# Weight sums of the first layer's seven-product down step, made ahead by GpSimd in the pool mixer's stage

## The chip, the core and the metric

The kernel runs on one core of a Trainium2 chip. The metric is the device time of one execution in microseconds. Three runs of the kernel before took 3083.82, 3086.56 and 3086.64 us; the median is 3086.56 us.

## What is computed

The reference is a two-layer transformer on 1024 tokens of width 1024, in float32. The parts that matter here, cut to their core:

```python
# first layer
h = rms_norm(x, attn_norm_w)
y_pool = pool_mixer(u_pool, pool_w, pool_scale) @ w_pool_br      # pool mixer
y_attn = nsa_attention(q, k, v, nsa_g, ...) @ w_attn_br          # 16 heads, 32-token query blocks
x = x + (merge_g[:, :, 0] * y_pool + merge_g[:, :, 1] * y_attn) @ w_o
h = rms_norm(x, ffn_norm_w)
u = causal_conv3(h @ w_up)                                       # 2 x 2752 columns
gate, val = split(u)
x = x + (silu(gate) * val) @ w_down                              # 2752 x 1024
# second layer: another mixer, then
h = h + square(relu(rmsnorm(h) @ w_ff1)) @ w_ff2                 # 4096 columns
```

## The kernel before, in words

Every large product is done to float32 accuracy in three matmuls: each operand is split in a high part (ScalarE, `whi`) and a remainder (VectorE or GpSimd, `wlo`), and `mm3` (L98) adds high x high, high x low and low x high. Splits of weights are at L93 and L94 (`unit`) and at L912 and L913 (`split`).

The feed-forward products use Strassen's method in the seven-product form of Winograd: a block of 512 rows of `w_down` or `w_ff2` is cut in quarters, and instead of eight quarter products there are seven, of sums of quarters. `down_fast` (L957) does this for four tiles of activations at once. It needs four sums of activation quarters on every call (`put(A, ...)`, L971, GpSimd) and four sums of weight quarters. There are two forms of it. Without `sums`, it loads the quarters, some of them twice (L967, L1025, L1029), and GpSimd forms the four sums of 128x1024 in place: at L1026 and L1028, and by two `put(B, ...)` at L971. With `sums`, it loads ready sums from a DRAM tensor at L1005, each just before its split. The first layer calls `down_fast` four times, without sums (in `phase_ffn1`, L1245, a loop over `n`; the rest of `w_down` is done by plain products). The second layer calls it seven times with sums.

Those sums of the second layer come from a generator, `weight_sums` (L921). It goes in steps, four to a weight group, each over a quarter's 256 columns. A step issues on SP's queue the stores of the step before (L942) and the loads of the step after (L933), and has GpSimd form four sums (L945 to L948) of 128x256. It has four tags of tiles with three buffers each. It is driven from the second layer's mixer by `next_step`, and its last step stores at L953.

The order of work is made by a planner when the program is built: each engine and each DMA queue has its own instruction list and works it off in order, and among what is ready in the planner's clock it takes what stands first in the program. `issue_after(ins)` adds one rule: what the block issues on the engine of `ins` goes behind `ins` in that engine's list. If `ins` is a DMA on SP's queue, the block's DMAs on SP stand behind it, and its GpSimd work is not bound by it.

SBUF memory is a stack of pools. A pool opened after another was closed begins where that one began; its tiles take their place in the order in which they are created. With `reuse_waits="tile"` a new tile waits for the last uses of those old tiles that lie on its bytes.

The stages around the change, in order: keys and values, queries (`phase_q`), the pool mixer (`phase_pool`, L232), the attention (`phase_attn`, L478). `phase_pool` has small tables (`rcnt` 256 bytes a partition, `pw` 2048, `psc` 16), then `yph` and `ypl` (16 KB each), and ends in a loop over eight output tiles: 24 matmuls, a copy by ScalarE to `yp` (four buffers) and a store to `yp_d` (L283). `phase_attn` opens its pool `pattn` with `wmask` (1280 bytes, a GpSimd DMA), `cmask` (1024 bytes, a GpSimd DMA), `fold` (768 bytes, set by VectorE at L490), `ftab` (512 bytes) and the query tiles `qt0` (4 KB, two buffers) and `qt1`. Its first step loads queries (L500), and runs `compressed`: scores on TensorE (L506), minima on VectorE, products on GpSimd (L512, L521, L526), a selection mask `sm`; then the masked scores (L566 on VectorE). TensorE's other work there is the gates (`gate_filler`): sixteen pieces of it, that is four halves of 24 matmuls each, stand in the program ahead of the first step, and the others are put by `issue_after` behind a matmul of the attention.

Of the kernel before, what the change touches and what calls it, by code (L numbers as in the profile page):

```python
# [22 lines left out]
P = 128  # L23
# [200 lines left out]
def early_gate(k, xT, z, n, g_d):  # L224

    nc = k.nc
    nc.scalar.activation(z, k.fm(k.unit(k.a["w_g"][n], 1024, P), *xT), AF.Tanh, scale=0.5)
    nc.gpsimd.tensor_scalar(z, z, 0.5, 0.5, op0=OP.mult, op1=OP.add)
    nc.sync.dma_start(g_d[n // 8, n % 8], z)


def phase_pool(k, xT, yp_d, g_d):  # L232

    nc, a = k.nc, k.a
    xh, xl = xT
    with k.tc.tile_pool(name="ppool", bufs=2, reuse_waits="tile") as p:
        rcnt = p.tile([P, 4, 16], F32, name="rcnt", bufs=1)
        nc.scalar.dma_start(rcnt, a["c_rcnt"])
        pw = p.tile([P, 4, P], F32, name="pw", bufs=1)
        nc.scalar.dma_start(pw, a["pool_w"])  # L240
        psc = p.tile([P, 4], F32, name="psc", bufs=1)
        nc.scalar.dma_start(psc, a["pool_scale"])
        yh = p.tile([P, 4, T], F32R, name="yph", bufs=1)
        yl = p.tile([P, 4, T], F32R, name="ypl", bufs=1)
        def pooled(g):
            acc = k.fm(k.unit(a["w_u"][g], 1024, P), xh, xl)
            u = p.tile([P, T], F32, tag="u", name=k.nm("u"), bufs=1)
            nc.scalar.activation(u, acc, AF.Copy)
            s = u
            for i in range(g + 1):  # L250
                d = 1 << i
                s2 = p.tile([P, T], F32, tag="s", name=k.nm("s"), bufs=4)
                nc.vector.tensor_tensor(s2[:, d:], s[:, d:], s[:, :T - d], op=OP.add)
                nc.gpsimd.tensor_copy(s2[:, :d], s[:, :d])
                s = s2
            wd = 2 << g
            nc.vector.tensor_tensor(s[:, :wd], s[:, :wd], rcnt[:, g, :wd], op=OP.mult)
            nc.vector.scalar_tensor_tensor(s, s, 1.0 / wd, u, op0=OP.mult, op1=OP.subtract)
            return g, s

        def mixed(g, s):
            for h in range(2):
                hs = slice(h * 512, h * 512 + 512)
                pa = k.bank("o")
                nc.tensor.matmul(pa, pw[:, g, :], s[:, hs], start=True, stop=True)
                nc.scalar.activation(yh[:, g, hs], pa, AF.Copy, scale=psc[:, g:g + 1])
                nc.vector.scalar_tensor_tensor(yl[:, g, hs], pa, psc[:, g:g + 1], yh[:, g, hs].bitcast(F32),
                                               op0=OP.mult, op1=OP.subtract)
        late = None
        for g in range(3, -1, -1):  # L270
            late, this = pooled(g), late
            if this:
                mixed(*this)
        for n in EARLY[1:]:
            early_gate(k, xT, p.tile([P, T], F32, tag="s", name=k.nm("z"), bufs=4), n, g_d)
        mixed(*late)
        for n in range(8):
            if n % 2 == 0:
                wb = k.unit(a["w_pool_br"][n // 2], 1024, P)
            acc = k.fm(wb, yh, yl, (3, 2, 1, 0), 4 * (n % 2))  # L280
            y = p.tile([P, T], F32, tag="s", name=k.nm("yp"), bufs=4)
            nc.scalar.copy(y, acc)
            nc.sync.dma_start(yp_d[n], y)  # L283


def rope_const(k, p):
# [634 lines left out]
def weight_sums(k, p, w, dst, n):  # L921

    nc = k.nc
    tt = nc.gpsimd.tensor_tensor
    steps = [(g, slice(h * 256, h * 256 + 256)) for g in range(n) for h in range(4)]

    def load(g, s):
        q = {}  # L930
        for name, (j, c) in (("b22", (1, 1)), ("b12", (0, 1)), ("b11", (0, 0)), ("b21", (1, 0))):
            q[name] = p.tile([P, 256], F32, tag=name, name=k.nm(name), bufs=3)
            nc.sync.dma_start(q[name], w[2 * g + j][c][:, s])  # L933
        return q["b11"], q["b12"], q["b21"], q["b22"]

    made, now = None, load(*steps[0])
    after = yield
    for i, (g, s) in enumerate(steps):
        with k.tc.issue_after(after.ins):
            if made:  # L940
                for d, x in made:
                    nc.sync.dma_start(d, x)  # L942
            following = load(*steps[i + 1]) if i + 1 < len(steps) else None
            b11, b12, b21, b22 = now
            tt(b12, b22, b12, op=OP.subtract)  # L945
            tt(b11, b12, b11, op=OP.add)
            tt(b21, b11, b21, op=OP.subtract)
            tt(b22, b22, b11, op=OP.subtract)  # L948
            made, now = [(dst[g, j][:, s], x) for j, x in enumerate((b12, b11, b21, b22))], following
        after = yield  # L950
    with k.tc.issue_after(after.ins):
        for d, x in made:
            nc.sync.dma_start(d, x)  # L953
    yield
# [183 lines left out]
    return h[:, 0], h[:, 1]  # L1138


def phase_ffn1(k, xT, acc, out_d):


    nc, a = k.nc, k.a
    t1, t2 = slice(0, 512), slice(512, T)
    with k.tc.tile_pool(name="pffn1", bufs=1, reuse_waits="tile") as p:
# [20 lines left out]
        def new_pair():  # L1167
            return p.tile([P, 2, T], F32, tag="uv", name=k.nm("uv"), bufs=2)
# [48 lines left out]
        us = [new_pair()]  # L1217
# [18 lines left out]
        for n in range(4):  # L1236
            us = []
            for j in range(4):
                if j % 2 == 0:
                    us.append(new_pair())  # L1240
                fast(1 + 4 * n + j, us[-1][:, j % 2], x)
                if n == 0 and j == 1:
                    with k.tc.issue_after(k.last_sum.ins):
                        swap_basis(k, acc, True, nc.vector)
            down_fast(k, p, us, [a["w_down"][1 + 2 * n + j] for j in range(2)], acc)  # L1245
        us = []
        for j in range(4):
            if j % 2 == 0:
# [92 lines left out]
def next_step(steps, after):  # L1341
    try:
        steps.send(after)
    except StopIteration:
        pass
# [553 lines left out]
@with_exitstack  # L1899
def transformer_kernel(ctx, tc, a, out, dbg=None):  # L1900
    k = K(ctx, tc, a, out, dbg)
    nc = tc.nc
    d = lambda shape, name, dt=F32: k.dram.tile(shape, dt, name=name)
    yp_d, g_d = d([8, P, T], "yp_d"), d([2, 8, P, T], "g_d")
    q_d, m_d = d([2, NT, P, 1024], "q_d"), d([8, P, 512], "m_d")
    x2_d, x3_d, y_d = (d([T, T], n) for n in ("x2_d", "x3_d", "y_d"))
    a_d = d([8, P, T], "a_d")
    v_d = d([T, 512], "v_d")

    qk_d = d([4, 2, 2, P, T], "qk_d")  # L1910
    xT = k.xopen()
    with tc.tile_pool(name="pkv", bufs=1, reuse_waits="tile") as p:
        kT = p.tile([P, 4, T], F32R, name="kT")
        V = p.tile([P, NT, 4, P], F32R, name="V")
        gates = p.tile([P, NT, 48], F32, name="gates")
        kcm = p.tile([P, 2, 2, 64], F32R, name="kcm")
        vcm = p.tile([P, 2, 2, 64], F32, name="vcm")
        phase_kv(k, xT, kT, V, gates, kcm, vcm, g_d)
        phase_q(k, xT, q_d)
        phase_pool(k, xT, yp_d, g_d)  # L1920
        k.close_psum()
        aT = phase_attn(k, kT, V, gates, q_d, kcm, vcm, a_d, xT, yp_d, g_d, m_d)
        k.open_psum(True)
    with tc.tile_pool(name="pacc", bufs=1, reuse_waits="tile") as p:
        acc = p.tile([P, NT, T], F32, name="acc1")
        xT = phase_wo(k, aT, g_d, m_d, acc)
        xT = phase_ffn1(k, xT, acc, x2_d)
    ws_d = d([7, 4, P, 1024], "ws_d")
    with tc.tile_pool(name="pahead", bufs=1, reuse_waits="tile") as p:
        k.ahead = weight_sums(k, p, a["w_ff2"], ws_d, 7)  # L1930
        next(k.ahead)
        yT, pre = phase_mix(k, xT, x2_d, y_d, v_d, qk_d)
    k.open_psum(True)
    p = ctx.enter_context(tc.tile_pool(name="px", bufs=1, reuse_waits="tile"))
    xT = p.tile([P, KT, T], F32R, name="xTh"), p.tile([P, KT, T], F32R, name="xTl")
    phase_res(k, "w_out", "ln_ff_g", yT, x2_d, x3_d, xT, (4, 5, 6, 7, 0, 1, 2, 3), pre)
    k.xclose()
    with tc.tile_pool(name="pacc2", bufs=1, reuse_waits="tile") as p:
        acc = p.tile([P, NT, T], F32, name="acc2")
        phase_ffn2(k, xT, x3_d, acc, ws_d)  # L1940
    k.close_psum()
# [141 lines left out]
```

## Time and profile before

| | |
|---|---|
| median of 3 runs | 3086.56 us |
| profiled execution | 3091.48 us, span 3089.7 us, mean granted TensorE clock 0.986 |
| TensorE busy | 2946.4 us, 95% of the span |
| VectorE, ScalarE, GpSimd busy | 2078.6 us (67%), 1375.3 us (45%), 1186.6 us (38%) |
| DMA | 293.06 MB, 95 GB/s in the mean |
| pool mixer's loop over output tiles | about 304 to 342 us of the span |
| attention | from 341 us |
| first layer's seven-product down steps | four, the first from about 1318 to 1350 us, the others each 122 us later |
| `weight_sums` of the second layer | 28 steps, 1863 to 2018 us |

The profile is one execution taken by the hardware profiler; its times are microseconds from the start of the span. PE is TensorE, DVE is VectorE, ACT is ScalarE, POOL is GpSimd, SP is SyncE, and SPq its DMA queue's issuing side.

### The profile page before, as it was taken

How to read it: one execution, taken by the hardware profiler on the slowest of the kernel's cores; microseconds unless marked ns; L12 is line 12 of the kernel's file. 1: busy time of each engine (PE TensorE's matmuls, PEld its weight loads, DVE VectorE, ACT ScalarE, POOL GpSimd, SP SyncE). 2: the span in 40 equal slices, each digit the busy share in tenths (PEclk: the TensorE clock that was granted, in tenths of full speed). 3: DMA queues.
4: the chain of work that ended last, by engine and by line, in shares of the span. 5: the costliest groups of instructions: out<-in, count | busy, mean ns of one | idle time of the engine just before them, and what ended most of it. 6: DMA issues, size and time to landing. Idle time of an engine off the chain costs nothing. (4 is left out here: it accounts for less than half of the span.)

```text
span 3089.7 us, 41918 instructions
## 1 busy us (share of the span) xinstructions
PE 2946.4 (95%) x14822; PEld 2442.4 (79%) x14822; DVE 2078.6 (67%) x4005; ACT 1375.3 (45%) x2447; POOL 1186.6 (38%) x1007
## 2 busy tenths in 40 slices
PE   8999999999999898999999999899989999999998
PEld 7887789889888776777877787676777878888876
DVE  8495277877777689687777873442465766666667
ACT  5243266666667234444434442332363453333333
POOL 3032355544455520344243405811331034444452
PEclk9999999999999998999999999999999999999999
DMA  3232412221232510111211127721783312222223
GB/s 135 77 112 91 154 42 74 68 67 52 88 100 93 194 62 29 55 62 41 67 57 53 64 96 235 233 77 40 185 217 113 112 62 76 75 75 76 75 75 136
DMA packets 157362, 293.06 MB, mean 95 GB/s; under 512 B 47969, under 2 KB 87393, under 8 KB 157153
## 3 DMA queue, kind: packets, MB, share of 16 engines
q1 hardware_dynamic: 150528, 274.72, 28.2%
q10 hardware_dynamic: 5760, 13.28, 1.3%
q8 instruction: 117, 1.92, 0.3%
q0 software_dynamic: 864, 2.39, 0.2%
q14 instruction: 93, 0.75, 0.1%
HBM read 225.09 MB, written 65.54 MB: 94 GB/s over the span
## 5 line engine op out<-in xcount | busy, mean ns | idle before, releaser
L912 ACT ACTIVATE whi<-wraw 128x1024 fp32r<-128x1024 f32 (+1 forms) x220 | 217.0, 991 | 349.1 <-PE up L101 148.6
L913 DVE TENSOR_TENSOR wlo<-wraw,whi 128x1024 fp32r<-128x1024 f32 x208 | 274.1, 1323 | 34.7 <-ACT whi L912 32.8
L577 POOL TENSOR_SCALAR e<-e,den,gates 128x640 f32<-128x640 f32 (+7 forms) x256 | 199.0, 790 | 215.4 <-DVE den L575 177.6
L101 PE MATMUL o<-wlo,whi 128*128 128x512 f32 x688 | 271.7, 395 | 10.0 <-DVE wlo L913 8.8
L102 PE MATMUL o<-whi,wlo 128*128 128x512 f32 x688 | 266.9, 393 | 12.8 <-DVE wlo L913 12.8
L100 PE MATMUL o<-whi,whi 128*128 128x512 f32 x688 | 253.6, 396 | 18.5 <-ACT whi L912 8.3
L990 DVE TENSOR_TENSOR acc<-acc,o 128x512 f32<-128x512 f32 x320 | 209.6, 679 | 20.7 <-PE o L102 20.3
L591 ACT ACTIVATE eh<-tr 128x512 fp32r<-128x512 f32 (+1 forms) x304 | 158.2, 537 | 121.3 <-PE o L595 79.4
L592 DVE TENSOR_TENSOR el<-tr,eh 128x512 fp32r<-128x512 f32 (+1 forms) x304 | 183.1, 615 | 41.2 <-ACT eh L591 35.5
L1105 POOL TENSOR_TENSOR wraw<-wraw,wraw 128x512 f32<-128x512 f32 x34 | 48.0, 1412 | 421.2 <-DVE wlo L913 319.1
L570 ACT ACTIVATE e<-e,m 128x640 f32<-128x640 f32 (+7 forms) x256 | 187.1, 733 | 34.5 <-DVE m L566 28.9
L93 ACT ACTIVATE whi<-wraw 128x1024 fp32r<-128x1024 f32 (+2 forms) x109 | 113.4, 1045 | 176.1 <-PE o L102 29.0
L565 PE MATMUL s<-kT,qt 128*128 128x320 f32 (+5 forms) x768 | 184.3, 347 | 4.1 <-DVE m L566 3.9
L100 PE MATMUL up<-xh,whi 128*128 128x512 f32 x432 | 171.7, 398 | 0.6 <-ACT xh L158 0.6
L100 PEld LDWEIGHTS o<-whi,whi 128*128 128x128 f32 x688 | 130.7, 190 | 52.0 <-ACT whi L912 10.7
L102 PE MATMUL up<-xh,wlo 128*128 128x512 f32 x432 | 170.2, 396 | 0.0
L101 PE MATMUL up<-xl,whi 128*128 128x512 f32 x432 | 169.8, 394 | 0.0
L102 PEld LDWEIGHTS o<-whi,wlo 128*128 128x128 f32 x688 | 129.6, 189 | 44.4 <-DVE wlo L913 17.9
L101 PEld LDWEIGHTS o<-wlo,whi 128*128 128x128 f32 x688 | 130.9, 190 | 42.0 <-DVE wlo L913 13.7
L94 DVE TENSOR_TENSOR wlo<-wraw,whi 128x1024 fp32r<-128x1024 f32 (+2 forms) x86 | 125.6, 1465 | 55.7 <-ACT whi L93 55.1
L587 PE MATMUL tr<-ident,e 128*128 128x128 f32 x1056 | 158.8, 274 | 3.1 <-ACT et L532 1.5
L595 PE MATMUL o<-el,V 128*128 128x256 f32 x528 | 146.3, 299 | 7.2 <-DVE el L592 6.6
(489 smaller groups left out, 8482.8 us busy)
## 6 DMA issues: line engine op xcount, KB each, us to landing
wraw<-in_w_ff_dram SPq DMA_DIRECT2D x57, 512.0 KB, 3.2
wraw<-in_w_up_dram SPq DMA_DIRECT2D x43, 512.0 KB, 3.2
b<-in_w_ff_dram SPq DMA_DIRECT2D x112, 128.0 KB, 3.2
ws_d<-b SPq DMA_DIRECT2D x112, 128.0 KB, 2.8
wraw<-ws_d SPq DMA_DIRECT2D x28, 512.0 KB, 3.2
wraw<-in_w_down_dram SPq DMA_DIRECT2D x26, 512.0 KB, 3.2
nqk<-qk_d SPq DMA_DIRECT2D x48, 256.0 KB, 5.9
wraw<-in_w_g_dram SPq DMA_DIRECT2D x16, 512.0 KB, 3.6
```

The costliest lines, as they stand in the source:

```text
L100: mm(out, sh, mh, start=first, stop=False, **kw)
L101: mm(out, sh, ml, start=False, stop=False, **kw)
L102: return mm(out, sl, mh, start=False, stop=last, **kw)
L565: nc.tensor.matmul(s[:, :w], qs[i][:, h, :], kT[:, br * 2 + g, ks], start=(i == 0), stop=(i == 1))
L570: nc.scalar.activation(e[:, :W], e[:, :W], AF.Exp, bias=m[:, n - 1:n], scale=-1.0, accum_out=den)
L577: nc.gpsimd.tensor_scalar(es[j][:, :W], es[j][:, :W], den[:, j:j + 1], gt[:, j, br:br + 1], op0=OP.mult, op1=OP.mult)
L587: nc.tensor.transpose(pt[:, x:x + P], es[i][:, (c + j) * P:(c + j + 1) * P], k.ident)
L591: nc.scalar.activation(eh[:, :w], pt[:, :w], AF.Copy)
L592: nc.vector.tensor_tensor(el[:, :w], pt[:, :w], eh[:, :w].bitcast(F32), op=OP.subtract)
L912: k.last_split = (k.nc.scalar.activation(pair[0], x, AF.Copy), (engine or k.nc.vector).tensor_tensor(pair[1], x, pair[0].bitcast(F32), op= ...
L913: (engine or k.nc.vector).tensor_tensor(pair[1], x, pair[0].bitcast(F32), op=OP.subtract))
L990: nc.vector.tensor_tensor(o, o, banks[t], op=op)
```

## The change

The sums of the four first-layer steps are made by the same generator, `weight_sums`, with four groups, so 16 steps, and kept in a new DRAM tensor `wd_d`. The first step's loads are issued ahead of the pool mixer's stage. Behind each of the first seven `yp_d` stores of the loop two calls of the generator are queued, behind the eighth three; 17 calls are 16 steps and the last stores. `down_fast` gets `wd_d[n]` and takes its form with sums. The generator's pool, `pahead1`, is opened before `phase_pool` and closed after it, so that the mixer's pool lies above its 12 tiles of 1 KB a partition.

```diff
@@ phase_pool
-            nc.sync.dma_start(yp_d[n], y)
+            sent = nc.sync.dma_start(yp_d[n], y)
+            for _ in range(3 if n == 7 else 2):
+                next_step(k.ahead, sent)
@@ phase_ffn1
-def phase_ffn1(k, xT, acc, out_d):
+def phase_ffn1(k, xT, acc, out_d, wd_d):
-            down_fast(k, p, us, [a["w_down"][1 + 2 * n + j] for j in range(2)], acc)
+            down_fast(k, p, us, [a["w_down"][1 + 2 * n + j] for j in range(2)], acc, False, wd_d[n])
@@ transformer_kernel
+    wd_d = d([4, 4, P, 1024], "wd_d")
-        phase_pool(k, xT, yp_d, g_d)
+        with tc.tile_pool(name="pahead1", bufs=1, reuse_waits="tile") as pa:
+            k.ahead = weight_sums(k, pa, a["w_down"][1:], wd_d, 4)
+            next(k.ahead)
+            phase_pool(k, xT, yp_d, g_d)
-        xT = phase_ffn1(k, xT, acc, x2_d)
+        xT = phase_ffn1(k, xT, acc, x2_d, wd_d)
```

The generator's core, which is not changed (`load` issues four DMAs of 128x256 on SP and takes the tags in the order `b22`, `b12`, `b11`, `b21`):

```python
for i, (g, s) in enumerate(steps):
    with k.tc.issue_after(after.ins):
        if made:
            for d, x in made:
                nc.sync.dma_start(d, x)
        following = load(*steps[i + 1]) if i + 1 < len(steps) else None
        b11, b12, b21, b22 = now
        tt(b12, b22, b12, op=OP.subtract)
        ...
    after = yield
```

## Rows read from the trace of the kernel before

**Rows 1.** Waits, engine PE, the first layer's feed-forward: total us, times, longest.
```profile
PE o L101 <- DVE wlo L913: 8.1, 8, 1.4
PE o L100 <- ACT whi L912: 6.3, 4, 1.6
...
PE o L102 <- DVE wlo L913: 2.7, 4, 0.7
PE o L100 <- DVE acc L990: 2.3, 4, 0.6
```
**Rows 2.** Waits, engine PE, the second layer's seven down steps, 2490 to 2980 us.
```profile
PE o L102 <- DVE wlo L913: 8.9, 7, 1.7
```
**Rows 3.** Timeline, POOL, first down step: start us, busy us, line, operation, tiles.
```profile
1323.40 2.41 POOL L1028 TENSOR_TENSOR wraw<-wraw,wraw 128x1024 f32<-128x1024 f32 x1
1330.29 9.10 POOL L971 TENSOR_TENSOR uv<-uv,uv 128x1024 f32<-128x1024 f32 x3 [4.48 <-DVE uv L1165]
1339.35 6.72 POOL L971 TENSOR_TENSOR wraw<-wraw,wraw 128x1024 f32<-128x1024 f32 x2
```
**Rows 4.** Timeline, DVE, the same step.
```profile
1323.45 2.37 DVE L1153 SCALAR_TENSOR_TENSOR uv<-ends,convp,uv 128x1 f32<-128x1 f32 x1
```
**Rows 5.** Timeline, SP's DMA issues, from the mixer's loop to the attention.
```profile
305.13 0.33 SPq L283 DMA_DIRECT2D yp_d<-yp  x1
...
336.43 5.92 SPq L283 DMA_DIRECT2D yp_d<-yp  x2
342.46 5.12 SPq L500 DMA_DIRECT2D qt<-q_d  x6
```
**Rows 6.** Timeline, PE: first and last matmul of a gate half, first scores.
```profile
340.75 0.39 PE L100 MATMUL f<-xh,whi 128*128 128x512 f32 x1
...
346.01 0.40 PE L102 MATMUL f<-xh,wlo 128*128 128x512 f32 x1
349.60 1.97 PE L506 MATMUL s<-kcm,qt 128*128 128x128 f32 x8 [3.19 <-DMA qt<-q_d]
```
**Rows 7.** Timeline, POOL, from the loop to the first attention step.
```profile
332.99 0.75 POOL L485 DMA_DIRECT2D wmask<-in_c_wmask_dram  x1
...
360.15 0.62 POOL L738 TENSOR_SCALAR z<-z 128x512 f32<-128x512 f32 x1 [5.41 <-ACT z L737]
360.75 1.04 POOL L521 TENSOR_TENSOR ec<-ec,dc 128x512 f32<-128x512 f32 x1
```
**Rows 8.** Timeline, DVE, from the loop's end to the first masked score.
```profile
341.02 0.22 DVE L490 MEMSET fold<- 128x192 f32 x1 [41.39 <-PE mm L102]
...
356.36 0.20 DVE L518 RECIPROCAL dc<-dc 128x8 f32<-128x8 f32 x1
...
366.18 0.69 DVE L566 CUSTOM_DVE_ANT_0 e<-s,sm 128x512 f32<-128x512 f32 x1 [1.17 <-POOL sm L548]
```
**Rows 9.** Timeline, SP's DMA issues, second layer's `weight_sums`: three steps between these.
```profile
1890.65 1.87 SPq L933 DMA_DIRECT2D b<-in_w_ff_dram  x4
...
1902.30 2.08 SPq L933 DMA_DIRECT2D b<-in_w_ff_dram  x4
```
**Rows 10.** Timeline, POOL, second layer's `weight_sums`: steps 1, 10 and 28.
```profile
1866.22 0.74 POOL L945 TENSOR_TENSOR b<-b,b 128x256 f32<-128x256 f32 x1 [80.11 <-DMA b<-in_w_ff_dram]
...
1907.72 0.73 POOL L945 TENSOR_TENSOR b<-b,b 128x256 f32<-128x256 f32 x1
...
2013.80 0.73 POOL L945 TENSOR_TENSOR b<-b,b 128x256 f32<-128x256 f32 x1 [2.06 <-DMA b<-in_w_ff_dram]
```
**Rows 11.** DMA issues: tiles, count, KB each, median us from issue to landing.
```profile
b<-in_w_ff_dram SPq DMA_DIRECT2D x112, 128.0 KB, 3.2
ws_d<-b SPq DMA_DIRECT2D x112, 128.0 KB, 2.8
```
**Rows 12.** Windows: busy us of PE, PEld, DVE, ACT, POOL; granted clock, DMA share, GB/s.
```profile
1890.00:1900.00 10.00, 10.00 (x45) 8.05 (x44) 1.50 (x4) 0.37 (x1) 7.44 (x11) 1.00 0.82 252
```
**Rows 13.** Timeline, ACT: it reads the fourth gate half.
```profile
373.26 0.60 ACT L737 ACTIVATE z<-f 128x512 f32<-128x512 f32 x1 [2.64 <-PE f L102]
```

## The prediction, made before the run

> **What bounds the kernel now.** I read the busy shares first: TensorE works 95% of the span, so a change counts only by what it does to TensorE's idle time. Next, TensorE's waits in the two stretches that the change touches. In the first layer's feed-forward the four seven-product down steps each show the same five stops: 8.1 + 6.3 + 2.7 + 2.3 = 19.4 us in all, 4.85 us a step [rows 1]. In the second layer, whose seven steps already read their sums from DRAM, all that recurs is 8.9 us over seven waits, 1.27 us a step [rows 2]. Then the timeline of one of the four steps, to see whose the stops are. GpSimd makes the weight sums in two pairs, two of 2.41 us and two in 6.72 us, around three sums of activations of 9.10 us [rows 3]. During the first pair a VectorE operation on 128x1 elements takes 2.37 us and ends with the GpSimd add (1325.82 against 1325.81) [rows 3, 4]; the accumulates queued behind it are late, and TensorE waits for one of their banks [rows 1]. The second pair stands before the last weight splits and the last stop.
>
> Last, the place where the work goes. The pool mixer's loop over eight output tiles is full of TensorE work and nearly empty elsewhere: VectorE waits 41.39 us there, up to 341.02 [rows 8]. Its stores leave the SP queue at 305.13 and, the eighth, after 336.43 (two in 5.92 us, so at about 342.0) [rows 5]. Right behind it stands the start of the attention, which is not full: TensorE runs one gate half (24 matmuls, 340.75 to 346.41), then waits 3.19 us for the first `qt` [rows 6].
>
> **What goes.** In each of four steps, four adds of 128x1024 and two second loads of weights; four splits now take loaded sums. The price is the stops, 19.4 us, less what remains. I take the second layer's remainder, 4 x 1.27 = 5.1: gain 14.3 us. Bounds: 19.4 if nothing remains; 9 if the stops of 1.6 us that wait for a split behind the three activation sums [rows 1, 3] and about one other remain, since VectorE has the convolution beside it here and not in the second layer. A loss is excluded as far as rows go: the same routine with two more loads a step makes no DMA wait of TensorE in seven steps [rows 2].
>
> The Trainium skill, SBUF — State Buffer, "Who interferes with whom", says that a VectorE instruction with two SBUF inputs and a GpSimd one that reads SBUF shut each other out, whole. The 2.37 us row agrees. By that rule VectorE gets back more than the stops tell, the gain is the upper end, 19.4 us, and the forecast would be 5 us lower, 3097.
>
> **What comes.** 16 steps; each is four loads and four stores of 128 KB on SP's queue and four adds of 128x256 on GpSimd. One load group goes out ahead of the stage. The rest are queued behind the loop's stores: two calls behind each, three behind the eighth. GpSimd: 4 x 0.74 = 2.95 us a step, 47 us in all, beside the gates' splits; by itself it would nearly keep up. SP: where the second layer's steps run undisturbed, three take from 1890.65 to 1902.30, 3.88 us each for eight issues [rows 9]. After 305.13 there are 31 groups of four, 15.5 x 3.88 = 60 us, with some 12 other issues of 0.33 us or more (4 us, of the kind in [rows 5]): last issue at 369, and with 2.8 us to land [rows 11], 372. So SP alone is some 30 us late at the end of a loop of 37 us. Buffers and data cost more: in the second layer the first ten steps' adds begin from 1866.22 to 1907.72, nine intervals, 4.61 us each; all 28 to 2013.80 make 5.47 us [rows 10]. I take 4.61, the row nearest to a place where VectorE is idle and GpSimd nearly so. Step 1's adds can begin at 305.13 + 1.9 (four issues) + 3.2 (landing) = 310.2; step 15's then at 310.2 + 14 x 4.61 = 374.7; with 2.95 of adds, 0.4 to issue and 2.8 to land, the last sum is in DRAM at **L = 381**. As a check, 31 groups are 16.3 MB; at the 252 GB/s of 1890 to 1900 [rows 12] that is 64.5 us without the loop's own traffic, so 370 at the earliest. Bounds of L: 354 (load 15 may leave only behind the eighth store at 342.0: 1.9 + 3.2 + 2.95 + 3.2, rounded up), and 393 with 5.47.
>
> **Why L is on the path.** Tiles take their memory in order of creation from the base of the stage before. The trace shows it: the attention's `wmask` DMA leaves at 332.99 with the loop still running, since with `cmask` it covers 2.3 KB, where `rcnt`, `pw` and `psc` (2.3 KB) lay; the next tile, `fold`, waits for the loop's last matmul, because it lies on `yph`, and the `qt` load leaves at 342.46 [rows 5, 7, 8]. After the change the base is that of the sums' pool, 12 tiles of 1 KB. `wmask`, `cmask`, `fold` and `ftab` end at 3.5 KB, the first `qt` at 7.5 KB: it lies on all three buffers of `b12`, so on steps 13, 14 and 15. The attention can't load its first query before step 15's stores have landed. Queued in front of it on GpSimd is the `wmask` DMA, and behind that everything that the attention wants of GpSimd.
>
> From issue to first score matmul took 342.46 to 349.60, 7.1 us; then 16.6 us to the first masked score on VectorE at 366.18 [rows 5, 6, 8]. In that chain a GpSimd product whose input was ready at 356.56 started at 360.75, behind a gate's operation [rows 7, 8]: 4.2 us that go when the gates are done by then. TensorE has four gate halves (some 5.5 us each) ahead of the first step, and the later ones are pinned behind a matmul of the attention; ScalarE reads the fourth at 373.26, so it ran behind this stretch [rows 13], and drawn into it covers 5.5 us. The cost is L + 7.1 - 349.6 - 4.2 - 5.5 = **L - 352.2**: 29 us at 381, 41 at 393, 2 at 354. A start at a lower clock after a stop was there before too, so I add nothing for it. Other things at nothing: the loop's matmuls (VectorE's 41.39 us without work say that no weight is split there [rows 8], and four `yp` buffers give each store three more tiles' time), and the memory by which the mixer's tiles shift; if a store of the loop held up a fifth tile, it would cost a tile's time, 37 / 7 = 5.3 us [rows 5].
>
> **Sum.** 29 - 14.3 = +15 us. The profiled execution took 3091.48 us (span 3089.7), so 3106 for a like one; it was 4.9 us above the median of the runs, 3086.56, and the same difference gives **3102 us**.
>
> **Rivals.** (1) Faster: the sums hide. One mechanism: the steps run at GpSimd's pace, 2.95 us, because issues and landings overlap, so that only the pin behind the eighth store counts, L = 354: cost 2, net -12, 3074 us. It decides at L = 366.5, where cost and gain are equal. For it: GpSimd and VectorE are free there. Against it: SP's 3.88 us a step [rows 9] and 252 GB/s [rows 12]. The same price holds if the first `qt` does not lie on the sums; `fold` and `wmask` speak against that. The Trainium skill, DMA: Bandwidth & Descriptors, "Issuing engines are not separate DMA queues", calls the time to initiate a DMA usually small beside the DMA itself; by it SP would be no limit and this rival's 3074 us would be near; the measured 8 issues in 3.88 us decide against it, and no chance is taken from it. (2) No difference: SP's floor, L = 372, cost 20, net +5.5, 3092; for it the pace of rows 9, against it that this held for three steps only. (3) Much slower: the 28-step pace, L = 393, cost 41, net +27, 3113; or the stops stay since the activation sums, not the weight sums, end last: gain 9 with L = 381, net +20, 3106, which stays in the main case. For it: with the loop's own traffic the DMA engines, at 0.82 in the undisturbed slice [rows 12], would be full.
>
> **Chances.** Main case (net +6 to +22) 0.47, rival 3 (above that) 0.25, rival 2 and its surroundings within 6 us 0.15, rival 1 0.13. A measurement of this kernel tells about 0.2%, 6 us, from no change. So faster 0.13, same 0.15, slower 0.72. The main case's own range is 3093 to 3109; to hold 0.8 the range takes in rival 2, part of rival 3 (up to 36 us) and the upper edge of rival 1: 3082 to 3123.
>
> **What would show it.** In the new trace: the last store of the sums' routine landing at 372 to 393, 30 us or more after the eighth store of the loop; the first `qt` load only after it; a TensorE wait of 20 us or more named for `qt` or a mask, in place of 3.19 us; adds of 0.74 us in the loop. In the four down steps, 1 to 2.5 us of stops each, no 2.37 us VectorE row, and no adds of 128x1024 on weights. The prediction is wrong if `qt` loads before the last sum has landed, if L is under 366, or if the down steps keep over 3 us of stops each.

## The result, and the profile after

The changed kernel took 3112.9 us (median of 4 runs, 3109.1 to 3121.1) against 3086.6 us for the kernel before on the same chip: a ratio of 1.0083 [1.0065, 1.0101], 26.3 us slower. The forecast was 3102 us, range 3082 to 3123. Its profiled execution took 3121.1 us (span 3119.3), 8 us above its median, so terms below are read inside a stage where that is possible.

Two lengths carry the reading. The first is the stretch of the down steps, from the first to the last of the forty `uv` products of VectorE. One line each from VectorE's timeline, kernel before, then after: line, operation, count, shortest/median/longest ns, first and last start.

```profile
L1165 DVE TENSOR_TENSOR uv<-ug,uv x40: 676/684/692, 1262.8 to 1816.4; 128x512 f32<-128x512 f32 x40
```
```profile
L1167 DVE TENSOR_TENSOR uv<-ug,uv x40: 677/684/692, 1298.5 to 1836.6; 128x512 f32<-128x512 f32 x40
```

553.6 us became 538.1: **the gain is 15.5 us**, 3.9 us a down step. The same stretch as a window (columns as in [rows 12]), before, then after:

```profile
1262.80:1816.40 553.60, 532.31 (x2295) 428.57 (x2294) 421.54 (x597) 243.51 (x315) 207.69 (x112) 1.00 0.18 60
```
```profile
1298.50:1836.60 538.10, 527.54 (x2294) 429.50 (x2293) 404.33 (x597) 242.61 (x315) 161.82 (x96) 1.00 0.21 69
```

TensorE's idle time fell from 21.3 to 10.6 us, and the modelled busy time of as many matmuls by another 4.8. The waits of TensorE in that stretch, after, in answer to [rows 1]:

```profile
PE o L100 <- ACT whi L914: 5.9, 4, 1.5
PE o L102 <- DVE wlo L915: 2.7, 4, 0.7
```

The stops for a bank and for the last weight splits (2.3 and 8.1 us) are gone; those behind the activation sums and for the last remainder stay, 2.15 us a step. VectorE's 128x1 operation, 2.37 to 2.46 us in each down step before (2.37 in [rows 4]), is never over 0.22 us now (VectorE's timeline, that line, after):

```profile
L1155 DVE SCALAR_TENSOR_TENSOR uv<-ends,convp,uv x40: 203/208/219, 1299.8 to 1836.4; 128x1 f32<-128x1 f32 x20, 128x2 f32<-128x2 f32 x20
```

The second length is the way into the attention. GpSimd's timeline after: the sums of step 1 and of step 15, and the first of attention's loads that GpSimd issues.

```profile
310.81 0.73 POOL L947 TENSOR_TENSOR b<-b,b 128x256 f32<-128x256 f32 x1
...
375.09 0.72 POOL L947 TENSOR_TENSOR b<-b,b 128x256 f32<-128x256 f32 x1 [2.16 <-DMA b<-in_w_down_dram]
...
382.90 0.75 POOL L487 DMA_DIRECT2D wmask<-in_c_wmask_dram  x1 [4.81 <-DMA wd_d<-b]
383.66 0.57 POOL L489 DMA_DIRECT2D cmask<-in_c_cmask_dram  x1
```

Fourteen intervals of 4.59 us; `wmask`, which waits for the last sum's store, leaves at 382.9 instead of 332.99 [rows 7]. SP's issues in the same stretch, in answer to [rows 5]: the loop's eighth store, the last sums and the `qt` loads.

```profile
368.59 0.38 SPq L283 DMA_DIRECT2D yp_d<-yp  x1
...
377.52 0.91 SPq L955 DMA_DIRECT2D wd_d<-b  x2
...
379.62 4.59 SPq L502 DMA_DIRECT2D qt<-q_d  x6
```

ScalarE's timeline after: an issue of its own stands in front of the gate's `z`, and that issue waits too.

```profile
377.92 0.33 ACTq L496 DMA_DIRECT2D ftab<-in_c_ftab_dram  x1
378.36 0.60 ACT L739 ACTIVATE z<-f 128x512 f32<-128x512 f32 x1 [36.18 <-POOL b L950]
```

So TensorE's stop after one gate half is named for `z`, not for `qt`. TensorE's waits, 300 to 420 us, after, where [rows 6] had 3.19 us for `qt`:

```profile
PE f L100 <- ACT z L739: 33.6, 2, 32.4
PE s L567 <- DVE ec L510: 5.4, 2, 5.0
PE s L567 <- DMA qt<-q_d: 1.6, 1, 1.6
PE s L508 <- DMA qt<-q_d: 0.6, 1, 0.6
```

VectorE's timeline after, in answer to [rows 8]: the first compressed score waits for `cmask`, and the first masked score begins at 410.14, 44.0 us later than before. The first line is that of the kernel before, where VectorE waited for the score.

```profile
350.75 0.42 DVE L507 TENSOR_TENSOR ec<-s,cmask 128x256 f32<-128x256 f32 x1 [9.09 <-PE s L506]
```
```profile
394.84 0.75 DVE L509 TENSOR_TENSOR ec<-s,cmask 128x256 f32<-128x256 f32 x2 [20.30 <-DMA cmask<-in_c_cmask_dram]
...
410.14 0.69 DVE L568 CUSTOM_DVE_ANT_0 e<-s,sm 128x512 f32<-128x512 f32 x1 [2.40 <-POOL sm L550]
```

On the way from the one to the other a GpSimd product, whose input VectorE had ready at 397.18, stands behind a gate's weight split (GpSimd's timeline after):

```profile
397.56 2.37 POOL L94 TENSOR_TENSOR wlo<-wraw,whi 128x1024 fp32r<-128x1024 f32 x1 [9.02 <-ACT whi L93]
...
400.48 1.04 POOL L514 TENSOR_TENSOR ec<-ec,mc 128x512 f32<-128x512 f32 x1
```

Windows after, columns as in [rows 12]: TensorE without work at a granted clock of 0.50 (the 1.2 GHz level), then the DMA engines full with everything that had been waiting.

```profile
360.00:370.00 10.00, 0.00 (x0) 0.00 (x0) 0.00 (x0) 0.00 (x0) 5.77 (x9) 0.50 0.89 292
...
380.00:390.00 10.00, 8.13 (x32) 6.15 (x30) 0.00 (x0) 1.06 (x1) 5.59 (x5) 0.84 1.05 329
390.00:400.00 10.00, 4.69 (x10) 3.04 (x11) 2.27 (x6) 1.54 (x2) 2.44 (x2) 0.50 0.54 143
```

### The profile page after: what moved, and what is told of

It is laid out like the page before. It is cut to its first block, busy times and chain, and to the rows that moved or that the text cites. A ratio compares the mean times of both kernels' runs of the same rounds, so it can differ in the third digit from the quotient of the medians.

```text
span 3119.3 us, 42223 instructions
## 1 busy us (share of the span) xinstructions
PE 2946.4 (94%) x14822; PEld 2444.4 (78%) x14822; DVE 2062.3 (66%) x4005; ACT 1373.5 (44%) x2447; POOL 1188.9 (38%) x1055
## 5 line engine op out<-in xcount | busy, mean ns | idle before, releaser
L992 DVE TENSOR_TENSOR acc<-acc,o 128x512 f32<-128x512 f32 x320 | 209.0, 679 | 21.6 <-PE o L102 21.3
```

The source lines that it names most:

```text
L992: nc.vector.tensor_tensor(o, o, banks[t], op=op)
```

## The experiments

Theory: the down steps give back some 14 to 16 us, and the place takes about 40, because attention's first loads come only when 16 steps of DMA traffic are through. Rivals: the memory on which attention's first tiles lie, the hold on ScalarE, and SP's issuing as such. Four sets, each beside runs of the kernel before (medians 3086.3, 3086.6, 3088.6, 3085.8); "median" is that of the kernel tried.

| run | median us | ratio to before | first masked score begins, later than before by |
|---|---|---|---|
| e2_gain | 3070.3 | 0.9954 [0.9939, 0.9970] | 3 us |
| e3_cost | 3127.0 | 1.0131 [1.0114, 1.0148] | 43 |
| e1_right | 3109.2 | 1.0073 [1.0055, 1.0091] | 34 |
| e4_ftab | 3112.1 | 1.0082 [1.0066, 1.0099] | 40 |
| e5_tables | 3109.6 | 1.0070 [1.0048, 1.0091] | 45 |
| e8_act | 3109.3 | 1.0068 [1.0046, 1.0089] | 42 |
| e11_narrow | 3115.4 | 1.0074 [1.0057, 1.0091] | 27 |
| e7_half | 3091.3 | 1.0015 [1.0000, 1.0030] | 16 |
| e6_query | 3095.3 | 1.0022 [1.0007, 1.0036] | 25 |
| e9_spread | 3093.9 | 1.0016 [1.0002, 1.0029] | 22 |
| e10_front | 3088.8 | 1.0004 [0.9989, 1.0018] | 18 |
| e12_attn | 3071.0 | 0.9958 [0.9940, 0.9976] | -3 |

**Gain and cost apart.**

```diff
# e2_gain: four steps only, all four down steps read them
-            down_fast(k, p, us, [...], acc, False, wd_d[n])
+            down_fast(k, p, us, [...], acc, False, wd_d[0])
-            k.ahead = weight_sums(k, pa, a["w_down"][1:], wd_d, 4)
+            k.ahead = weight_sums(k, pa, a["w_down"][1:], wd_d, 1)
# e3_cost: all steps, none read
-            down_fast(k, p, us, [...], acc, False, wd_d[n])
+            down_fast(k, p, us, [...], acc)
```

> Leaves out three quarters of the sums: only the first group's four steps are made, and all four down steps of the first layer's seven-product form read that one group's sums. This prices the gain by itself: four steps behind the first two or three mixer outputs are long done when attention begins. Prediction as made: 14.3 us below before (bounds 9 to 19.4), 3072 us. By the trace of the changed kernel, in which 2.2 us of each down step's stop is left: 10.7 us below before, 3076 us. Rival: if the four steps cost something where they stand, the time is over 3080 us.

> All 16 steps of sums are made and stored, but the down steps don't read them and make their own as the kernel before does (the sums are work for nothing here). This prices the cost by itself. By the prediction's sum: 29 us over before, 3116 us. By the trace of the changed kernel (29.6 us of added TensorE idle time in the profile, plus the 10.7 that the down steps gave): 37 to 40 us over before, 3124 to 3127 us. Rival: if part of the loss lies in the down steps' new load of the sums rather than ahead of attention, the time is under 3116 us.

Measured: 16.1 us under before (14.2 by the ratio), and 40.7 us over (40.4 by the ratio). 40.7 - 16.1 = 24.6 against the 26.3 of the two together, so the two terms add up. The forecast's gain of 14.3 stands; its cost of 29 was 11 to 12 too low. In e2_gain the stretch of `uv` products is 538.1 us long, as in the changed kernel:

```profile
L1167 DVE TENSOR_TENSOR uv<-ug,uv x40: 678/684/692, 1259.5 to 1797.6; 128x512 f32<-128x512 f32 x40
```

**Is it memory?** Two edits, and the one on ScalarE's hold:

```diff
# e1_right: the sums at the other end of SBUF
-        with tc.tile_pool(name="pahead1", bufs=1, reuse_waits="tile") as pa:
+        with tc.tile_pool(name="pahead1", bufs=1, side="right", reuse_waits="tile") as pa:
# e4_ftab: in phase_attn, and allocated ahead of all stages
-        ftab = p.tile([P, NT, 16], F32, name="ftab", bufs=1)
+        ftab = k.ftab
# e5_tables: as e4, and the same for wmask, cmask and fold
```

> Only the place of the sums' tiles is changed: they lie at the other end of SBUF, so that none of attention's first tiles (the tables, the fold, the q tiles) is laid over them; steps, order and the down steps' use of the sums stay. Theory A (memory: attention's first tiles wait for the last sum because they lie on its tile): the fold runs at about 341 again, ScalarE is free for the gates, the q loads stand where the queue lets them; most of the 37 us that the changed kernel pays goes, and the time is 3078 to 3092 us. Rival B (SP's queue: the q loads stand behind the sums' loads and stores in SP's order, whatever lies where): the q loads are still issued at 375 to 380 in the profile, the gates alone get their cover back, and the time is 3098 to 3106 us. Rival C (the extra 16 steps' DMA traffic itself delays the loads): nothing changes, 3110 to 3116 us.

> Only the table ftab, whose load ScalarE issues, is moved to memory of its own, off the sums' tiles. In the changed kernel that issue stood at 377.9 us in ScalarE's order with z of the first gate half behind it, and TensorE stopped 32.4 us. Theory (the issue held ScalarE, so the gates didn't cover the wait): the gate halves run from about 341 without the stop, some 12 to 16 us of matmuls come ahead of the wait for the sums, and the time falls by 6 to 14 us against the changed kernel, to 3099 to 3107 us. Rival (the gates are only moved, the tables and q tiles that follow end the wait just the same, and what follows them is unchanged in length because VectorE's and GpSimd's parts of attention's start set it): no change, 3110 to 3116 us.

> All four of attention's first tables (ftab, wmask, cmask, fold) get memory of their own; of attention's first tiles only the q tiles still lie on the sums' tiles, and their loads still stand behind the last sums' stores in SP's order. Theory Q (SP's order sets it: the q loads come at about 379, and what follows them, not the memory, is the cost): the q loads are issued at 378 to 381 again, the wait for cmask (5 us of TensorE's, in the changed kernel) goes, and the time is 3104 to 3110 us. Rival M (the tables' late waits were the larger part): under 3100 us. Rival N (as with ftab alone: gates and tables only move work about): 3110 to 3116 us.

None gave back more than 3.7 us; e1_right lies between what its rivals B and C asked. In e1_right `fold` ran early and `wmask` left at 374.2, but the `qt` loads still left at 378.01, since they stand behind the sums in SP's order (SP's timeline):

```profile
377.40 0.50 SPq L955 DMA_DIRECT2D wd_d<-b  x1
378.01 0.46 SPq L502 DMA_DIRECT2D qt<-q_d  x1
```

Theory A fell by its number. This run doesn't clear memory altogether: `ftab` still waited for a load of the sums, so some tile of the attention lay on them there too. In e4_ftab ScalarE was free, and TensorE did another gate half (windows 340 to 360: 11.4 us of matmuls against 6.6), yet the time stayed. Its waits of TensorE, 335 to 425 us:

```profile
PE s L508 <- DMA qt<-q_d: 33.5, 1, 33.5
PE s L567 <- DVE ec L510: 5.7, 2, 5.4
```

So ScalarE's hold, the longest wait in the changed kernel, was no cause here: without it the same stop stands one product further on, under the name of `qt`. In e5_tables VectorE no longer waits for `cmask` either, but the `qt` loads leave only at 385.89, and the first masked score comes no earlier. From the end of the first masked score to the first `uv` product it is 887.7 us in the changed kernel and 889.4 in e4_ftab; 889.5 and 892.3 where little was late (e2_gain, e12_attn); 896.0 in the profiled run of before. So what delays the first masked score delays the rest nearly one for one. That gate halves done early are lacking later would explain it, but one half is some 5.5 us and these profiles differ by 8, so it is not shown.

**What paces the steps?**

```diff
# e8_act: the sums' stores on ScalarE's queue
-                    nc.sync.dma_start(d, x)
+                    nc.scalar.dma_start(d, x)
# e11_narrow: as e8, 128 of each 256 columns, and the down steps as in e3
```

> The sums' stores are issued by ScalarE instead of SP; the same bytes, steps and order else. It parts SP's issuing (3.9 us of its order in each step of 4.6) from the transfers (283 to 292 GB/s at a DMA share of 0.84 to 0.89). Theory Q1 (SP's issuing sets the pace): a step falls to 3.2 to 3.8 us (POOL's 2.9 us of adds, or 1 MB at 329 GB/s), the last sum lands 13 to 22 us earlier, and the time is 3091 to 3101 us. Rival Q2 (the transfers set the pace, whichever engine issues them): the pace stays at 4.4 to 4.7 us, 3108 to 3116 us. Rival Q3 (ScalarE's copies of the mixer outputs are held up behind the stores, and TensorE with them): slower than the changed kernel, over 3116 us.

> Leaves out half of each sum: the steps, their issues and their order are the changed kernel's, the stores on ScalarE, but each load, add and store has 128 columns instead of 256; the down steps don't read the sums and make their own, so that the time is to be held against that of all sums made and not used (3127 us, or 3123 with the 3.6 us that ScalarE's stores gave). Theory D (the transfers set the pace of 4.5 to 4.8 us a step): half the bytes, the pace falls to about 3 us, the last sum lands some 20 to 25 us earlier, and the time is 3098 to 3106 us. Rival I (the number of issues, or the rounds of load, add and store by their fixed delays, set the pace): over 3115 us.

e8_act went as Q2 has it: 3.6 us better, no more. With half of the issues on another queue the last sums left at 379 to 382 (376 to 378 in the changed kernel). Once the loop was over, ScalarE did nothing but issue (its timeline):

```profile
346.59 32.16 ACTq L944 DMA_DIRECT2D wd_d<-b  x32
```

Eight steps in 32.2 us, 4.0 a step, while four issues take 1.9 us of a queue; over the same fourteen intervals as above GpSimd's sums come 4.83 us apart (310.67 to 378.35), against 4.59. But ScalarE's copies of the mixer's outputs stood behind the stores, one for 12.0 us, and the loop's last copy began at 346.5 instead of 341.0. So this run mixes two effects, too. The windows from 320 to 370, after, then e8_act:

```profile
320.00:370.00 50.00, 26.58 (x115) 21.11 (x113) 0.00 (x0) 4.05 (x4) 30.40 (x44) 0.79 0.85 279
```
```profile
320.00:370.00 50.00, 29.71 (x120) 23.57 (x120) 0.00 (x0) 8.11 (x8) 29.98 (x38) 0.83 0.93 307
```

The DMA engines, not SP, are the nearest to full. This agrees with the Trainium skill, DMA: Bandwidth & Descriptors, "Issuing engines are not separate DMA queues": what ScalarE issues runs on the same DMA engines, and only the time to issue is saved. e11_narrow was to settle it and didn't. With half the bytes the last sums leave from 362.6 on, instead of 375.8 in the changed kernel or 379.1 in e8_act. That is the same number of issues at 3.6 us a step, where theory D asked for 3. The time is 11.6 us below that of e3_cost (13.9 when each is taken beside its own runs of before, 17.6 by the ratios), less than the 21 to 29 of theory D, at the edge of rival I. This run mixes things as well: ScalarE's copies stood behind its stores (waits of 8.8, 7.3 and 12.3 us). That transfers limit the pace, and not issues alone, is supported, and not shown to be the whole of it.

**Fewer steps, and other places.**

```diff
# e7_half: two groups, one step a store; down steps 2 and 3 as before the change
-            for _ in range(3 if n == 7 else 2):
+            for _ in range(2 if n == 7 else 1):
# e6_query: in phase_q, the pool opened ahead of it
+                for _ in range(2 if (g, t) == (1, 7) else 1):
+                    next_step(k.ahead, sent)          # behind each store of q
# e9_spread: 6 behind the copies of v, 8 behind every second store of q, 2 in the mixer's loop
# e10_front: 8 behind every second store of q, 4 behind mixed(), 4 in the mixer's loop
```

> Half of the sums: only the first two groups' eight steps are made, one behind each mixer output's store (two behind the eighth), and the last two down steps make their own as before. Theory Q with a pace of 4.6 us a step: a step fits between two stores that are 5.3 to 5.6 us apart, the last sum lands at 345 to 350, ahead of 352, and the cost is 0 to 6 us; the gain is half of 14 to 16: 3079 to 3086 us. Rival (each step costs its own share, 40.7 / 16 = 2.5 us, whether or not it ends in time): 3086.5 + 20 - 7.5 = 3099 us.

> The same 16 steps stand in the query stage instead, one behind each of its 16 stores of q, so that all sums have landed before the pool mixer begins; nothing is in SP's order ahead of attention's q loads that was not there before. Theory Q (the cost is that attention's loads stand behind the steps): the cost goes and the gain of the down steps stays, 14 to 16 us under before: 3070 to 3076 us. Rival L (GpSimd's 64 adds of 0.73 us and VectorE, which is busy 47 of 50 us in that stage, hold each other up, and TensorE, which is busy throughout there, is starved): part or all of 47 us comes back, 3080 to 3115 us.

> All 16 steps, thinly spread: six behind ScalarE's copies of v in the key and value stage (where GpSimd is busy 1 of 50 us in the trace of before and the DMA share is 0.3), eight in the query stage (one behind every second store of q), two behind the first two mixer outputs; the last sums are stored behind the third. Theory D (the cost is the steps' transfers standing together in front of loads that something waits for, about 1.4 MB a step at 283 to 292 GB/s; spread over 240 us they fit): the cost goes but for VectorE's share in the query stage, at most half of the 7.6 us that 16 steps there took from TensorE; 14 to 16 less 0 to 4: 3071 to 3077 us. Rival L (GpSimd's adds or the transfers hold up the key, value and query stages): over 3080 us.

> All 16 steps, spread without the key and value stage: eight in the query stage, four behind the pool mixer's four group copies, four behind the first four mixer outputs, the last sums stored behind the fifth. Theory D: nothing is left ahead of attention's loads by 340 us, and the query stage loses up to 4 us: 3071 to 3078 us. Rival L as above, with the mixer's own inputs (u, 9.8 us of TensorE's when all 16 steps stood in the query stage) held up again: 3080 to 3090 us.

All four missed their theory. e7_half: half the steps give half the gain (the stretch is 545.8 us, 7.8 less than before), but the `qt` loads still leave at 356 and the first masked score begins 16 us late. In e6_query the query stage, which is full on TensorE and nearly so on VectorE, pays. Its waits of TensorE, and the copy of `u` on ScalarE's timeline (the profiled run took 3112.3 us, 17 above its median):

```profile
PE mm L100 <- ACT u L248: 9.8, 1, 9.8
...
PE tr L411 <- DVE qT L414: 4.8, 5, 1.7
```
```profile
276.18 0.34 ACTq L238 DMA_DIRECT2D rcnt<-in_c_rcnt_dram  x1
...
279.46 1.02 ACT L248 ACTIVATE u<-mm 128x1024 f32<-128x1024 f32 x1 [7.85 <-DMA rcnt<-in_c_rcnt_dram]
```

Here the pool mixer's `u` takes attention's part: its copy stands on ScalarE behind the issue of the mixer's table `rcnt`, which left at 276.18 (251.73 in the kernel before). It is the hold of `ftab` again, and here TensorE had nothing else to do. What `rcnt` itself waited for, no run separates. Thinner spreading shrinks this and doesn't end it. TensorE from 150 to 300 us, before, then e10_front:

```profile
150.00:300.00 150.00, 150.00 (x702) 121.46 (x701) 114.94 (x228) 53.15 (x85) 42.84 (x43) 1.00 0.28 98
```
```profile
150.00:300.00 150.00, 140.49 (x646) 112.33 (x645) 121.09 (x221) 45.60 (x79) 86.06 (x90) 0.98 0.53 178
```

Before, TensorE has no gap there, so 9.5 us of gaps come out as time. The loop's first store leaves at 319.2 in e10_front, 328.7 in e9_spread and 331.5 in e6_query instead of 305.1: 14, 24 and 26 us late. Less the 15.5 of the down steps that is -1, +8 and +11; the medians lie 0.2, 5.3 and 8.7 us over before.

**A place with room.** The forecast's argument, that the steps cost because attention's first loads wait behind them, points to the attention itself: 600 us long, DMA share 0.16 to 0.35, and gates that fill TensorE.

```diff
# e12_attn: in gate_filler; no steps in phase_pool
-            nc.sync.dma_start(g_d[n // 8, n % 8][:, s], z)
+            sent = nc.sync.dma_start(g_d[n // 8, n % 8][:, s], z)
+            halves += 1
+            if halves == 6:
+                k.ahead = weight_sums(k, p, a["w_down"][1:], k.wd_d, 4, "b12")
+                next(k.ahead)
+            elif halves > 6:
+                next_step(k.ahead, sent)
# in weight_sums: two buffers for b12, three for the others, so that attention's pool holds them
```

> All 16 steps stand in attention, one behind each store of a half of the gates from the seventh half on (from about 450 to 700 us, a half each 13 to 36 us apart; the DMA share there is 0.16 to 0.25, GpSimd is busy 24 to 29 of 50 us, and TensorE has the gates as filler). Theory P (place: a step costs nothing where the DMA engines are idle and no load of a later stage stands behind it; the gain of the down steps then stays whole): 14 to 16 us below before, less up to 5 for the turns that VectorE and GpSimd take: 3071 to 3079 us. Rival L (64 adds of 0.73 us stand in GpSimd's order ahead of the subtractions and sums of the softmax, and VectorE slows beside them; attention's chain of steps is fed by both): up to 47 us come back, 3080 to 3118 us.

3071.0 us, 14.8 under the 3085.8 of before beside it (13.0 by the ratio) and 42 under the changed kernel: theory P. **It beats both kernels.** The sums (one of four lines of GpSimd's timeline, fifteen of its sixteen adds) now stretch over 260 us; the stretch of down steps keeps its 538.2 us; and a window in the attention shows the added load beside a full TensorE:

```profile
L955 POOL TENSOR_TENSOR b<-b,b x15: 732/737/750, 451.1 to 713.0; 128x256 f32<-128x256 f32 x15
```
```profile
L1175 DVE TENSOR_TENSOR uv<-ug,uv x40: 679/684/692, 1255.9 to 1794.1; 128x512 f32<-128x512 f32 x40
```
```profile
500.00:550.00 50.00, 49.95 (x331) 45.23 (x329) 38.40 (x114) 33.49 (x69) 34.88 (x38) 1.00 0.43 138
```

## Why the prediction was right, and where its sizes were off

- **Direction and mechanism: right.** The last sum landed after the loop, attention's first loads came behind the steps, TensorE stood for over 20 us, and the gain did not pay for it.
- **The sum: inside the range, by rival 3's number.** The measured +26.3 us lies above the main case's +6 to +22 and next to rival 3's +27. But rival 3's mechanism, a pace of 5.47 us and L = 393, did not come: the pace was the main case's, and the cost behind L was larger.
- **Gain, 14.3 us (9 to 19.4): 15.5.** The remaining stops were put at 1.27 us a step and are 2.15, so the waits alone gave back 10.7; the 4.8 that the same matmuls run shorter was in no term. The two errors all but cancel, which is luck. The upper end that went with the Trainium skill's "Who interferes with whom" (SBUF — State Buffer) did not come: its sign is there, 2.37 us down to at most 0.22, its price isn't.
- **L = 381: 382.9.** Step 15's adds were forecast for 374.7 and began at 375.09. The pace, taken from [rows 10], held. That SP's 3.88 us a step alone is the floor is not borne out: with half of the issues moved away the pace was no better (e8_act), and with half the bytes and all the issues it fell to 3.6 us (e11_narrow).
- **Why L is on the path: half right.** The memory argument describes what waits, but SP's order alone does the same: with the sums elsewhere, `qt` still left at 378 (e1_right). No run put the `qt` loads ahead of the steps with the memory apart, so order and memory are not priced one by one. One of the forecast's signs of being wrong came true by a little: the first `qt` load left at 379.62, 3.3 us ahead of L, right behind the last issues of stores; what waited for the last store's landing was `wmask`, and `cmask` behind it.
- **Cost = L - 352.2: the step that was mis-sized.** It put 7.1 + 16.6 - 4.2 = 19.5 us from L to the first masked score; it was 410.1 - 382.9 = 27.2. The first scores began at 387.33, 4.4 us behind L instead of 7.1. From them to the first use of `cmask` it was 7.5 us instead of 1.15: `cmask` left only at 383.66, and VectorE could use it at 394.84, 11.2 us later (4.8 us from issue to landing before), in the slice where the DMA engines carry 329 GB/s. The 4.2 us that were taken off for GpSimd went where the forecast had them and came back elsewhere: one product waited 3.3 us (397.18 to 400.48), and `sm` 1.3. And the forecast took off 5.5 us for a gate half drawn into the wait; one more half drawn in gave nothing (e4_ftab). 1.9 + 7.7 + 5.5 = 15 too little by this profile; the medians say 40.4 - 29 = 11, so that some of the 5.5 may have come back after all. No run separates it.
- **The low clock, "so I add nothing":** it was 0.50 twice, at 350 to 380 and at 390 to 400, and some fifteen gate matmuls began 0.43 us apart instead of 0.23, 3 us in all; before it was nine of them, 1.8 us, in the slice from 350 to 360 (granted clock 0.71). The first of the two stretches did not make the scores late, since TensorE then still waited 0.6 us for `qt`; how much of the 7.7 is the second, no run separates.
- **A stop named for `qt` or a mask:** it was named for `z`, since ScalarE issues `ftab` in line with its arithmetic. Not foreseen, and by e4_ftab without price here.

## What to carry to other kernels

Work made ahead is free only where nothing that comes soon is queued behind it and the engines that it uses, the DMA engines among them, have room to the stage's end: look at who loads next, not only at who is idle now. When a stage's start is late, count how late its first consumer is, nearly one for one, and don't take off fill-in work before a run shows that it isn't only moved. And price the gain and the cost in two separate runs before judging the sum: here a bad place hid a gain that a good place kept nearly whole. And the longest wait in a list need not be a cause: freed here, it came back under the next name.

## What was not expected of the hardware

A DMA issue in a compute engine's list holds that engine's arithmetic while the issue waits: 36.2 us on ScalarE for a table of 512 bytes a partition, without price while `qt` was late anyway (e4_ftab), and 9.8 us of TensorE's where a table of the mixer did the same (e6_query). Loads that are let go together land late together: `cmask` took 11.2 us from issue to use beside the `qt` loads, against 4.8 us to landing before. Two queues instead of one for the same bytes raised the rate only from 279 to 307 GB/s.
